# Twenty of the low-part subtractions of a decoder trunk's weights issued on GpSimd instead of VectorE

## The chip, the cores and the metric

The kernel runs on one core of one Trainium2 chip. The metric is the device time of one execution in microseconds (us); the time of a kernel is the median of its runs. One execution is also recorded by the hardware profiler, and the profile's spans, groups and waits come from that one.

Five queues work side by side: TensorE (PE, with its weight loads as PEld), VectorE (DVE), ScalarE (ACT), GpSimd (POOL) and SyncE (SP), which here only issues transfers. Each queue runs its instructions strictly in its own order; semaphores order them between queues.

## What is computed

The input is a residual stream of 512 tokens by 1024 channels. Layer 0 mixes by causal average pooling, layer 1 by stick-breaking attention with 16 heads of 64 channels; each layer adds a squared-ReLU MLP (1024 to 4096 to 1024), with an RMS norm before and after each part. The part that the change touches is layer 1's attention:

```python
h = rms_norm(x, mix_pre_g[layer])
q = jnp.matmul(h, w_q[j])                        # 1024 x 1024
kv = jnp.matmul(rms_norm(x, kv_norm_g), w_kv)    # k and v, 1024 x 1024 each
a[t, s] = sigmoid(z) * prod_{s<j<t} (1 - sigmoid(z_tj))   # z = q k^T / 8, strictly causal
m = jnp.matmul(o, w_o[j])                        # o = a v, 1024 x 1024
```

All data are float32.

## The kernel before, in words

**Split products.** TensorE's operands are held as two parts of a narrower float format (fp32r): `hi` is the value rounded by ScalarE's cast, and `lo` is the value minus `hi`. A product is three matmuls: hi x hi, hi x lo and lo x hi (`mm3`, lines 208 to 211, and `up_block`, lines 530 to 536). So every weight tile has to be split before TensorE can use it.

**How a weight comes in.** `weight` (lines 106 to 121) makes one tile of 128 x 1024. It takes one of two `raw` buffers, has SyncE issue the load (512 KB, L108), for the q, k and v weights has GpSimd multiply the tile in place by a norm gain in two halves of 128 x 512 (L130), has ScalarE cast `hi` (L118), and has an engine subtract `lo = raw - hi` (L120). That engine is VectorE, unless the weight's key is in the set `ON_POOL` (L43, looked up in `make`, L154), in which case it is GpSimd. In the kernel before, the set holds four of the first MLP's up weights: 0, 1, 2 and 4. The `raw` buffer is free for the load after next only when its `lo` has been made. The parts `h` and `l` lie in four buffers each (L150).

**What orders the work.** Weights are queued in the order in which they will be used (`want`, lines 171 to 184), and `fill` (lines 157 to 162) makes the next one at set places of the program if fewer than four are waiting. In attention, `weight` queues its cast behind ScalarE's latest instruction of the main work and its `lo` behind VectorE's latest (`later`, lines 110 to 120): `issue_after(ins)` places behind `ins` those instructions of the block that run on the engine of `ins`. A planner (`schedule_with_timeline_sim`, L887) then fixes the order of each queue when the kernel is compiled, from durations that it assumes; nothing is reordered at run time.

**The attention stage.** Its program order is written out by hand in `ATT_ORDER` (lines 49 to 53). Eight pairs of heads pass through it, overlapped: P projects keys and queries of a pair (two `up_block`s of 24 matmuls, then `kl` and `q` low parts on VectorE, L694 and L703); S multiplies queries by keys, has ScalarE make two sigmoids `u` and `w` (L746, L750), VectorE scan `u` into `e` (L752, 128 x 1280) and multiply `w` by `e` (L756); T has TensorE transpose `w` (L770) and splits the result into `ah` and `al` (L188, L189); A multiplies by the values (L780) and sums into `o` (L786, L787), which is split as `ohl`. V makes values (L209 to L211 with `xnh`, then L654, L655) and O multiplies finished pairs by the o weights (L209 to L211 with `ohl`). The order of the weights in attention is: v0, k0, q0, k1, q1, v1, k2, q2, k3, q3, o0, o1, k4, q4, v2, k5, q5, k6, q6, v3, k7, q7, o2 to o7; each v is two tiles.

The scan reads two SBUF tensors, and so do `w x e`, the `ohl` split and `lo = raw - hi`; the other VectorE operations of the stage read one operand from PSUM.

Of the kernel before, what the change touches and what calls it, by code (L numbers as in the profile page):

```python
# [25 lines left out]
PAIRS = HEADS // 2  # L26
# [14 lines left out]


ON_POOL = {("up", 0, j) for j in (0, 1, 2, 4)}  # L43

# [15 lines left out]
def trunk(ctx, tc, x, consts, gcol, grow, pw, wup, wdn, wq, wk, wv, wo, out):  # L62
# [43 lines left out]
    def weight(src, tiles, scaled=None, on=nc.vector):  # L106
        raw = wts.tile([P, D], F32, tag="raw", bufs=2, name=name("raw"))
        nc.sync.dma_start(raw, src)  # L108

        def later(engine):  # L110
            return tc.issue_after(behind[engine].ins) if engine in behind else nullcontext()

        if scaled is not None:
            with later("pool"):
                scaled(raw)
        hi, lo = tiles
        with later("act"):
            nc.scalar.copy(hi, raw)  # L118
        with later("dve"):
            on.tensor_tensor(out=lo, in0=raw, in1=hi.bitcast(F32), op=ALU.subtract)  # L120
        return hi, lo
# [19 lines left out]
    def place(k):  # L141

        if k[0] == "dn":
            return [dn_pool[0].tile([P, D], F32R, tag="w", bufs=8, name=name(x)) for x in "hl"]
        if k == ("o", 6):
            both = att_pool[0].tile([P, 2, D], F32R, tag="v", bufs=2, name=name("w"))
            return [both[:, 0], both[:, 1]]
        if k == ("o", 7):
            return [att_pool[0].tile([P, NSEG], F32R, tag="w", bufs=2, name=name(x))[:, :D] for x in "hl"]
        return [wts.tile([P, D], F32R, tag=f"w{x}", bufs=4, name=name(x)) for x in "hl"]  # L150

    def make():
        k, src, scaled = queue.pop(0)
        on = nc.gpsimd if k in ON_POOL else nc.vector  # L154
        made[k] = weight(src, place(k), scaled, on)
# [735 lines left out]
```

## Time and profile before

| | us |
|---|---|
| median of three runs | 994.51 (992.58 to 997.41) |
| the profiled execution, its own time | 996.64 |
| its span, first to last instruction | 994.8 |
| TensorE busy in the span | 954.4 |
| VectorE busy | 780.6 |
| ScalarE busy | 557.0 |
| GpSimd busy | 252.2 |

The profiled execution took 996.64 us, of which 994.8 us lie between its first and its last instruction. Busy time is the time in which an engine had an instruction under way. A row of the timeline gives start and duration in us, the engine, the line of the kernel, the operation, output and inputs with their shapes, and in brackets how long the engine sat idle before it and what ended that. A row of a group gives the count, the busy time in all and the mean of one in ns. `in_wk`, `in_wq`, `in_wv` and `in_wo` are the weights in memory; `l` and `h` are the parts of a weight; `ps` is any PSUM tile.

### The profile page before, as it was taken

Reading aid. Unit: us, or ns where it says so; the run is one execution under the profiler, and the core shown is the slowest. Engines: PE = TensorE matmul, PEld = TensorE weight load, DVE = VectorE, ACT = ScalarE, POOL = GpSimd, SP = SyncE. Lnnn points to the kernel's source line nnn. Section 1 sums busy time; section 2 is a strip of 40 time slices with the busy share of each in tenths; the row PEclk is TensorE's granted clock in tenths of the full one; section 3 lists DMA queues with packets and bytes.
Section 4 is the critical chain, followed back from the end, with each engine's and each line's share of the span. In section 5 each row is a group of like instructions: output and inputs, shape, how many; then the busy total and the mean of one; then the engine's idle time right before and its main releaser. Section 6 shows DMA issues by size and latency. Waiting matters only on the chain.

```text
span 994.8 us, 12988 instructions
## 1 busy us (share of the span) xinstructions
PE 954.4 (96%) x4823; PEld 810.8 (82%) x4823; DVE 780.6 (78%) x1067; ACT 557.0 (56%) x1005; POOL 252.2 (25%) x238
## 2 busy tenths in 40 slices
PE   7898999999999999999999999989999999999997
PEld 5896888888888888888788988788888888888886
DVE  5987788878877747488688889989778878888636
ACT  5656546456455446566667576658556455464532
POOL 1642202112021147241252300436212021121103
PEclk8998999999999999999999999999999999999999
DMA  7254323323232230112222221144323233231202
GB/s 267 85 162 135 106 86 107 109 103 106 85 111 81 85 127 22 62 45 64 64 73 69 64 72 65 65 148 149 110 102 111 84 125 105 85 127 64 64 22 85
DMA packets 26991, 94.50 MB, mean 95 GB/s; under 512 B 3120, under 2 KB 3504, under 8 KB 26928
## 3 DMA queue, kind: packets, MB, share of 16 engines
q1 hardware_dynamic: 26928, 93.68, 28.2%
q8 instruction: 38, 0.62, 0.2%
q14 instruction: 25, 0.20, 0.1%
HBM read 91.57 MB, written 2.10 MB: 94 GB/s over the span
## 4 chain that ended last, share of the span: by engine, by line
PE 76%; DVE 8%; ACT 4%; POOL 3%; issue 2%; DMA 1%; POOLq 0%; DVEq 0%; ACTq 0%
PE ps L456 26%; PE ps L535 13%; PE ps L536 13%; PE ps L534 13%; PE ps L209 3%; PE ps L210 2%; PE ps L211 2%; DVE e L752 2%; PE ps L780 1%; DVE l L120 1%; PE ps L770 1%; POOL y L234 1%; DMA xn<-in_wdn 1%; ACT h L118 1%; DVE x L240 1%
## 5 line engine op out<-in xcount | busy, mean ns | idle before, releaser
L535 PE MATMUL ps<-xnl,h 128*128 128x512 f32 (+1 forms) x712 | 262.0, 369 | 4.1 <-DVE xnl L189 4.1
L536 PE MATMUL ps<-xnh,l 128*128 128x512 f32 (+1 forms) x712 | 262.1, 369 | 0.5 <-DVE l L120 0.5
L534 PE MATMUL ps<-xnh,h 128*128 128x512 f32 (+1 forms) x712 | 261.0, 369 | 0.0
L120 DVE TENSOR_TENSOR l<-raw,h 128x1024 fp32r<-128x1024 f32 x101 | 128.8, 1276 | 48.5 <-ACT h L118 48.3
L456 PE MATMUL ps<-w,s 128*128 128x512 f32 x672 | 163.4, 394 | 2.1 <-ACT s L188 1.5
L535 PEld LDWEIGHTS ps<-xnl,h 128*128 128x128 f32 x712 | 134.8, 189 | 26.1 <-DVE xnl L189 4.3
L536 PEld LDWEIGHTS ps<-xnh,l 128*128 128x128 f32 x712 | 134.8, 189 | 22.8 <-DVE l L120 0.7
L456 PEld LDWEIGHTS ps<-w,s 128*128 128x128 f32 x672 | 127.2, 190 | 31.1 <-ACT s L188 2.7
L534 PEld LDWEIGHTS ps<-xnh,h 128*128 128x128 f32 x712 | 134.2, 190 | 21.9
L473 DVE TENSOR_TENSOR y<-ps,y 128x512 f32<-128x512 f32 x180 | 120.1, 688 | 40.5 <-PE ps L456 39.3
L118 ACT CAST h<-raw 128x1024 fp32r<-128x1024 f32 x105 | 110.4, 1053 | 63.9 <-PE ps L535 32.4
L456 PE MATMUL ps<-w,r 128*128 128x512 f32 x504 | 124.3, 390 | 2.4 <-DVE r L189 2.4
L188 ACT CAST w<-t 128x512 fp32r<-128x512 f32 x112 | 69.2, 622 | 80.8 <-PE ps L456 61.0
L456 PEld LDWEIGHTS ps<-w,r 128*128 128x128 f32 x504 | 94.7, 188 | 22.4 <-DVE r L189 2.8
L404 POOL TENSOR_TENSOR s<-r,r 128x256 f32<-128x256 f32 x28 | 28.2, 1008 | 323.9 <-ACT r L490 323.9
L130 POOL TENSOR_TENSOR raw<-raw,gc 128x512 f32<-128x512 f32 x48 | 69.9, 1477 | 145.7 <-DMA raw<-in_wv 68.9
L188 ACT CAST w<-xn 128x512 fp32r<-128x512 f32 x56 | 34.9, 624 | 90.1 <-PE ps L456 80.0
L189 DVE TENSOR_TENSOR w<-t,w 128x512 fp32r<-128x512 f32 x112 | 76.5, 705 | 0.7 <-ACT w L188 0.7
L188 ACT CAST s<-s 128x512 fp32r<-128x512 f32 x56 | 34.6, 620 | 45.6 <-POOL s L405 37.6
L189 DVE TENSOR_TENSOR s<-s,s 128x512 fp32r<-128x512 f32 x56 | 42.5, 763 | 22.0 <-ACT s L188 17.5
L189 DVE TENSOR_TENSOR r<-r,r 128x512 fp32r<-128x512 f32 (+1 forms) x60 | 47.2, 789 | 11.7 <-ACT r L188 11.6
L752 DVE TENSOR_TENSOR_SCAN e<-u,begin 128x1280 f32<-128x1280 f32 x16 | 47.5, 2968 | 8.7 <-ACT u L746 8.5
(138 smaller groups left out, 1577.9 us busy)
## 6 DMA issues: line engine op xcount, KB each, us to landing
raw<-in_wup SPq DMA_DIRECT2D x64, 512.0 KB, 3.5
xn<-in_wdn SPq DMA_DIRECT2D x42, 512.0 KB, 3.6
spare<-in_wdn SPq DMA_DIRECT2D x14, 512.0 KB, 4.1
raw<-in_wdn SPq DMA_DIRECT2D x8, 512.0 KB, 3.5
raw<-in_wv SPq DMA_DIRECT2D x8, 512.0 KB, 3.4
raw<-in_wk SPq DMA_DIRECT2D x8, 512.0 KB, 3.5
raw<-in_wq SPq DMA_DIRECT2D x8, 512.0 KB, 3.5
raw<-in_wo SPq DMA_DIRECT2D x8, 512.0 KB, 3.5
```

Of the source, the lines that this page charges most:

```text
L118: nc.scalar.copy(hi, raw)
L120: on.tensor_tensor(out=lo, in0=raw, in1=hi.bitcast(F32), op=ALU.subtract)
L130: nc.gpsimd.tensor_tensor(out=v[:, h], in0=v[:, h], in1=g[:, h].broadcast_to((P, n // 2, D // n)), op=ALU.mult)
L188: latest["act"] = nc.scalar.copy(hi, src)
L189: latest["dve"] = nc.vector.tensor_tensor(out=lo, in0=src, in1=hi.bitcast(F32), op=ALU.subtract)
L209: nc.tensor.matmul(dst, ah, bh, start=start, stop=False)
L456: nc.tensor.matmul(bank, r[:, a], w_[:, NS[b]], start=start and q == 0 and k == 0, stop=q == 1 and k == 2, skip_group_check=True,)
L473: nc.vector.tensor_tensor(out=part, in0=bank, in1=part, op=ALU.add)
L534: nc.tensor.matmul(pu[:, cols], wh[:, k, :], xnh[:, k, cols], start=k == 0, stop=False)
L535: nc.tensor.matmul(pu[:, cols], wh[:, k, :], xnl[:, k, cols], start=False, stop=False)
L536: nc.tensor.matmul(pu[:, cols], wl[:, k, :], xnh[:, k, cols], start=False, stop=k == KC - 1)
L752: nc.vector.tensor_tensor_scan(out=e[:, ::-1], data0=u[:, 1:][:, ::-1], data1=begin[:, ::-1], initial=0.0, op0=ALU.mult, op1=ALU.max,)
```

## The change

One line adds twenty keys to the set: the k and q weights 1 to 7 (fourteen tiles) and the o weights 0 to 5 (six tiles). The `lo` of each is then issued on GpSimd's queue, in which the gain multiplications also stand, and no longer on VectorE's. Keys k0, q0, o6, o7, all v weights and the MLP weights are left as they are. Since the block around the subtraction names VectorE's latest instruction, it places nothing in front of a subtraction that runs on GpSimd.

```diff
@@ -41,6 +41,8 @@
 
 
 ON_POOL = {("up", 0, j) for j in (0, 1, 2, 4)}
+
+ON_POOL |= {(x, i) for x in "kq" for i in range(1, PAIRS)} | {("o", i) for i in range(6)}
```

## The prediction

> **What bounds the kernel now.** I read the shares of the engines first, then the attention stage as one stretch of the table by stage (its columns after the length: PE, PEld, DVE, ACT and POOL busy, each with its count, then clock and DMA), since the twenty weights are split between 409 and 614 us, and then TensorE's waits in that stretch (total, times, longest).
>
> ```profile
> PE 954.4 (96%) x4823; PEld 810.8 (82%) x4823; DVE 780.6 (78%) x1067; ACT 557.0 (56%) x1005; POOL 252.2 (25%) x238
> ```
> ```profile
> 405.00:632.00 227.00, 217.77 (x1251) 190.28 (x1249) 186.94 (x192) 145.39 (x288) 55.69 (x37) 0.99 0.21 69
> ```
> ```profile
> PE ps L209 <- DVE kl L694: 1.9, 2, 1.4
> PE ps L780 <- ACT ah L188: 1.7, 1, 1.7
> PE ps L780 <- DVE al L189: 1.6, 2, 0.9
> PE ps L738 <- DVE q L703: 1.0, 1, 1.0
> ```
>
> TensorE bounds the kernel: 96% of the span, and 217.8 of the stage's 227.0 us. So 9.2 us can be won there at most, however much VectorE is relieved. The longest waits end with VectorE, but not with a weight's subtraction: with main work that stands in the same queue. VectorE is busy for 186.9 us of the stage and GpSimd for 55.7 us, so there is room on GpSimd; the question is what of VectorE's relief reaches TensorE's gaps.
>
> **What is removed and added.** First the subtraction on either engine (min, median and max in ns):
>
> ```profile
> L120 DVE TENSOR_TENSOR l<-raw,h x101: 1193/1225/2304, 16.1 to 952.4; 128x1024 fp32r<-128x1024 f32 x101
> ```
> ```profile
> L120 POOL TENSOR_TENSOR l<-raw,h x4: 2366/2466/2807, 25.2 to 65.3; 128x1024 fp32r<-128x1024 f32 x4
> ```
>
> VectorE loses 20 x 1.225 = 24.5 us. GpSimd gets 20 x 2.466 = 49.3 us and stands at 55.7 + 49.3 = 105 us of 227. Neither sum is TensorE's.
>
> **The two engines stop each other**, and this decides how much of the 24.5 us VectorE keeps:
>
> ```profile
> 647.43 2.30 DVE L120 TENSOR_TENSOR l<-raw,h 128x1024 fp32r<-128x1024 f32 x1
> ```
> ```profile
> 646.93 1.72 POOL L249 TENSOR_TENSOR y<-x,spare 128x512 f32<-128x512 f32 x1 [0.87 <-DVE x L240]
> ```
>
> GpSimd's operation ran to 646.93 + 1.72 = 648.65. VectorE's subtraction, recorded from 647.43, ended at 649.73: 1.08 us after GpSimd let go, nearly the whole of its own 1.2. It had stood still until then. The Trainium skill states this as a rule (SBUF — State Buffer, section "SBUF: two separate sides"): a GpSimd operation and a VectorE operation with two SBUF inputs share one port pair, held for a whole instruction, and the loser fully blocks. The trace agrees in these two rows.
>
> What this costs VectorE in the stage today is the mean above the median (means of the stage first, then medians):
>
> ```profile
> L752 DVE TENSOR_TENSOR_SCAN e<-u,begin 128x1280 f32<-128x1280 f32 x16 | 47.5, 2968 | 8.7 <-ACT u L746 8.5
> L120 DVE TENSOR_TENSOR l<-raw,h 128x1024 fp32r<-128x1024 f32 x29 | 37.9, 1310 | 9.2 <-ACT h L118 9.1
> L756 DVE TENSOR_TENSOR w<-w,e 128x1280 f32<-128x1280 f32 x16 | 26.1, 1633 | 0.8
> ```
> ```profile
> L752 DVE TENSOR_TENSOR_SCAN e<-u,begin x16: 2807/2825/3486, 421.2 to 605.7; 128x1280 f32<-128x1280 f32 x16
> ```
> ```profile
> L756 DVE TENSOR_TENSOR w<-w,e x16: 1472/1490/2081, 424.7 to 609.0; 128x1280 f32<-128x1280 f32 x16
> ```
> ```profile
> L130 POOL TENSOR_TENSOR raw<-raw,gc x36: 1035/1042/3553, 414.3 to 567.7; 128x512 f32<-128x512 f32 x36
> ```
>
> Scans 16 x 0.143 = 2.3 us, products 16 x 0.143 = 2.3, subtractions 29 x 0.085 = 2.5: 7.1 us for 36 x 1.042 = 37.5 us of gain multiplications, 0.19 us for each us of GpSimd. For 49.3 us more that is 9.4 us. A wait for the rest of one operation also grows with its length, 2.466 against 1.042, so at most 9.4 x 2.37 = 22 us. VectorE keeps between 24.5 - 22 = 2 and 24.5 - 9.4 = 15 us.
>
> **Where it meets TensorE's gaps.** `lo` can start on GpSimd where ScalarE has ended `hi`:
>
> ```profile
> L118 ACT CAST h<-raw x29: 1042/1051/1216, 408.2 to 626.6; 128x1024 fp32r<-128x1024 f32 x29
> ```
>
> Of the twenty that are moved I found most to end where VectorE works on PSUM, which a subtraction on GpSimd doesn't disturb; there 1.2 us leave a queue that TensorE doesn't wait for, worth 0. Five places have a gap of TensorE or a scan beside them.
>
> *First, 518 to 525 us* (k5 and q5): the largest gaps, as pieces of the chain of waits and then on TensorE.
>
> ```profile
> 519.09 1.23 DVE l L120
> ...
> 521.67 1.05 ACT h L118
> 522.75 1.23 DVE l L120
> ```
> ```profile
> 523.65 0.49 PE L780 MATMUL ps<-ah,v 128*128 128x512 f32 x1 [1.67 <-ACT ah L188]
> 525.08 0.50 PE L780 MATMUL ps<-al,v 128*128 128x512 f32 x1 [0.94 <-DVE al L189]
> ```
>
> Both 1.23 us leave this chain, 2.5 at most, and no scan runs here. Late next is ScalarE, whose `ah` casts stand behind its cast of q5's `hi`: only the first subtraction moves that. TensorE gets 0.7 to 2.5 us; I take 1.3, one subtraction and a little.
>
> *Second, 413 to 418 us* (q1).
>
> ```profile
> 414.44 1.95 DVE l L120
> 416.42 0.70 DVE q L703
> 417.17 0.58 issue
> 417.75 1.05 ACT h L118
> ```
> ```profile
> 414.27 3.02 POOL L130 TENSOR_TENSOR raw<-raw,gc 128x512 f32<-128x512 f32 x2 [16.76 <-DMA raw<-in_wv]
> ```
>
> L703 stands behind the subtraction, and the wait of 1.0 us on L703 above is this one; it can go. But GpSimd's gain multiplication of the next weight began at 414.27, just when q1's `lo` would take GpSimd. If `lo` is first, the next `hi` (the cast at 417.75) is up to 2.47 - 1.23 = 1.2 us late, and ScalarE's sigmoids and the scans behind it. Between 1.0 won and 1.2 lost I take 0.
>
> *Third, 447 to 454 us* (q2): the one place where TensorE waits for the `lo` of a weight that is moved at more than 0.2 us.
>
> ```profile
> 446.59 1.22 ACT L118 CAST h<-raw 128x1024 fp32r<-128x1024 f32 x1
> ```
> ```profile
> 448.94 3.32 DVE L752 TENSOR_TENSOR_SCAN e<-u,begin 128x1280 f32<-128x1280 f32 x1
> 452.19 1.19 DVE L120 TENSOR_TENSOR l<-raw,h 128x1024 fp32r<-128x1024 f32 x1
> ```
> ```profile
> 453.44 0.50 PE L536 MATMUL ps<-xnh,l 128*128 128x512 f32 x1 [0.51 <-DVE l L120]
> ```
>
> `hi` is there at 447.8. If GpSimd has its turn before the scan, `lo` is early and 0.5 us goes; if the scan is first, `lo` runs from 452.3 to 454.7 instead of to 453.4, and 1.3 us is lost. I take the middle, 0.4 lost.
>
> *Fourth, 476 to 487 us* (o0, o1).
>
> ```profile
> 476.21 1.05 ACT L118 CAST h<-raw 128x1024 fp32r<-128x1024 f32 x1
> ```
> ```profile
> 478.42 0.67 DVE L189 TENSOR_TENSOR ohl<-o,ohl 128x512 fp32r<-128x512 f32 x1
> 479.00 1.49 DVE L756 TENSOR_TENSOR w<-w,e 128x1280 f32<-128x1280 f32 x1
> ```
> ```profile
> 485.68 0.50 PE L210 MATMUL ps<-l,ohl 128*128 128x512 f32 x1 [0.21 <-DVE l L120]
> ```
>
> o0's `hi` ends at 477.3, inside a scan; GpSimd's turn comes when that ends, at 478.4, and pushes the product back by 2.47 us, while 1.22 us leave the queue behind it. TensorE takes o1's `lo` at once, so its 2.47 instead of 1.22 us adds up to 1.2. At worst 1.4 us is lost; at best the 1.2 us that leave VectorE are won, less a later o1, 0.7. I take 0.6 lost, as both longer durations stand in its way.
>
> *Fifth, 605 to 611 us* (o4).
>
> ```profile
> 605.90 1.05 ACT L118 CAST h<-raw 128x1024 fp32r<-128x1024 f32 x1 [3.19 <-PE ps L211]
> ```
> ```profile
> 605.70 2.82 DVE L752 TENSOR_TENSOR_SCAN e<-u,begin 128x1280 f32<-128x1280 f32 x1
> ```
> ```profile
> 610.55 0.66 PE L770 MATMUL ps<-ident,w 128*128 128x128 f32 x4 [0.17 <-DVE w L756]
> ```
>
> `hi` ends at 607.0, again inside a scan that runs to 608.5. GpSimd then has 608.5 to 611.0, so the product behind it ends 1.49 us later, at 612.4, and TensorE, which was served at 610.55, waits 1.9 us more; the subtractions of o4 and o5, which no longer stand behind the product, give back 1.2 to 2.4. Between 1.2 won and 0.6 lost I take 0.3 lost.
>
> **Transfers.** A `raw` buffer is freed by `lo` (SyncE's own waits):
>
> ```profile
> SPq L108 <- DVE l L120: 195.1, 27, 19.6
> ```
>
> All loads of the stage hang on L120. Where `lo` starts right behind `hi`, the load after next goes out 1.2 us later; where VectorE's queue held it (q2: 4.4 us from `hi` to `lo`), earlier. The cover is the four weights made ahead, so I cost it at 0; without cover it is 1.2 us a weight. The gain multiplications now share their queue with a `lo` in front; beyond the second place I cost that at 0 too, as GpSimd is free for 122 of 227 us.
>
> **Sum:** -1.3 + 0 + 0.4 + 0.6 + 0.3 = 0.0 us, with ends at -(2.5 + 1.0 + 0.5 + 0.7 + 1.2) = -5.9 and -0.7 + 1.2 + 1.3 + 1.4 + 0.6 = +3.8. The profiled execution stays at its 996.6, which is 2.1 us above the median; against the median of 994.5 the ends are 988.6 and 998.3. I put the time at 995.0, half a us up, because GpSimd's queue stands in front of ScalarE's casts in more places than these.
>
> **Rivals.** *Slower: GpSimd's turn comes inside the scans.* The mechanism is the standstill above, which the skill's rule of the whole instruction makes general. Scan, product, scan and product of a pair of heads offer a turn at each boundary; a `lo` that takes one costs the chain 2.47 us where 1.23 leave it, so 1.24 each and 2.5 a pair with both weights. It decides where the second product ends less than 2.5 us ahead of TensorE's transposes. With three pairs like the one at 610 us, and the bad end of the third place: 3 x 2.5 + 1.3 = 8.8 us, 1003.3. For it: scans already reach 3486 and multiplications 3553 ns. Against: TensorE waits for a product 0.2 us in the whole stage, so most pairs have a lead.
>
> *Faster: the subtractions were the last straw for VectorE.* All good ends, 5.9 us: 988.6; all gaps closed, 9.2 us: 985.3. For it: most of the long waits end with VectorE. Against: ScalarE or a scan is late next in four of the five places.
>
> *The planner orders the queues anew*, as an instruction has changed its engine. No row has a price for that. It widens both rivals: at best to the closed gaps, -9.2 us, at worst I take the 9.4 us that VectorE's new waits may reach by their average price, plus the 2 us by which single runs lie off the median, +11.
>
> The skill also advises against the change as such (GPSIMD Engine Reference, section "Engine selection": elementwise work with two inputs belongs on VectorE, GpSimd taking about twice as long). The rows agree on the factor, 2466 against 1225 ns; by the advice alone the sum would be a loss, by busy time GpSimd stays far from a bound.
>
> **Chances.** Within 0.5% of 994.5, about what a measurement of this kernel can tell from no change (989.5 to 999.5): 0.40, the forecast. Slower: 0.38, at 1003.3. Faster: 0.22, at 988.6. The range for 8 in 10 runs from 986.5, a little above all gaps closed, to 1006, 994.5 + 11.
>
> **What would show it.** Right: L120 on VectorE falls from 101 to 81 and on GpSimd rises from 4 to 24, with a mean above 2.5 us; scans and products have larger means than 2968 and 1633; the gaps at k5 and q5 shrink by about 1 us, those beside o0 and o4 grow. Wrong: TensorE's idle time in the stage is under 5 us (the faster rival), or over 14 us with waits that end in L756 or L770 (the slower one); if they end in `h`, `l` or a sigmoid, GpSimd's queue has become what the weights wait for.

## The result, and the profile after

The changed kernel takes 998.46 us (median of 12 runs, 996.60 to 1003.85) against 994.36 us for the kernel before (12 runs, 991.80 to 998.28). The ratio is 1.0044, with a 95% interval of 1.0025 to 1.0063: slower by 4.1 us. That lies inside the range of the prediction and just inside its band of 0.5% around no change, but twelve runs of each do tell it from no change. Timed again later, the same kernel stood at 1.0057 [1.0041, 1.0073]. The profiled execution took 998.91 us, 2.3 us more than that of before.

The shares of the engines on the page of the changed kernel, then the attention stage as one stretch of the table by stage (PE, PEld, DVE, ACT and POOL busy, each with its count, then clock and DMA):

```profile
PE 952.8 (96%) x4823; PEld 810.2 (81%) x4823; DVE 761.7 (76%) x1047; ACT 556.5 (56%) x1005; POOL 305.2 (31%) x258
```
```profile
405.00:632.00 227.00, 213.21 (x1216) 186.35 (x1215) 165.81 (x169) 144.31 (x286) 105.94 (x57) 0.98 0.21 68
```

VectorE was relieved of 186.94 - 165.81 = 21.1 us in the stage, and GpSimd stands at 105.9 us, as worked out. But TensorE did less in the same 227 us: its idle time rose from 9.2 to 227 - 213.21 = 13.8 us. The length of the stage is taken from here on from the matmul that ends TensorE's wait for the norm (`xnh`, at 397.82 us, before at 399.39) to the one that ends its wait for the next norm (`xnl`): it is 255.9 us, before 252.7.

TensorE's waits in the stage show where (total, times, longest, in us). Lines of the changed kernel are two higher than before: L122 is the subtraction, L772 and L782 the matmuls that were L770 and L780.

```profile
PE ps L538 <- POOL l L122: 3.6, 1, 3.6
PE ps L211 <- DVE kl L696: 3.5, 3, 1.2
PE ps L772 <- DVE w L758: 1.6, 2, 1.3
PE ps L212 <- POOL l L122: 1.4, 1, 1.4
PE ps L772 <- DVE q L705: 1.1, 1, 1.1
PE ps L536 <- ACT w L752: 1.0, 1, 1.0
```

Two of these are new in kind: TensorE waits for a low part that GpSimd makes, for 3.6 and 1.4 us. The first alone is larger than any wait in the stage before. The chain of waits around it (start, length, what), in the changed kernel:

```profile
439.45 3.46 DMA raw<-in_wk
...
444.56 3.55 POOL raw L132
448.12 3.57 POOL l L122
451.69 0.04 issue
451.73 0.80 PE ps L538
452.53 0.43 PE ps L536
...
454.66 0.32 PE ps L538
454.98 0.23 PE ps L536
```

The wait is for q2's low part (L122). That subtraction stood behind a gain multiplication (L132) of the *next* weight, k3, in GpSimd's queue. Both were stretched: the second half of the multiplication took 3.55 us, where the median of before was 1.042, and the subtraction 3.57 instead of 2.47. VectorE's scan and product ran beside them. The kernel before had k3's multiplication stretched as well, where no subtraction stood behind it on GpSimd:

```profile
444.24 5.34 POOL L130 TENSOR_TENSOR raw<-raw,gc 128x512 f32<-128x512 f32 x2 [1.87 <-DMA raw<-in_wk]
```

Behind the gap TensorE's matmuls take 0.43 us a piece until 454.98, and then 0.23: the granted clock fell to half.

Where TensorE stands in the stage is seen from the first matmul of each S step, in us after the matmul at which the stage's length begins (from the timelines of one execution each):

| pair | 0 | 1 | 2 | 3 | 4 | 5 | 6 | 7 |
|---|---|---|---|---|---|---|---|---|
| before | 17.8 | 41.2 | 68.1 | 99.7 | 126.4 | 151.1 | 175.2 | 196.7 |
| after | 15.1 | 38.0 | 69.4 | 102.2 | 130.6 | 156.3 | 180.3 | 201.4 |
| lo_first | 15.1 | 38.1 | 64.2 | 98.6 | 125.5 | 149.6 | 173.5 | 195.6 |
| lo_first_half | 16.6 | 39.6 | 65.7 | 97.7 | 125.0 | 149.2 | 173.2 | 195.5 |
| no_lo | 15.1 | 38.2 | 64.4 | 94.1 | 119.9 | 144.5 | 168.6 | 189.9 |

The changed kernel is 3.2 us *ahead* at pair 1, and 1.3 us late at pair 2: 4.5 us are lost at one weight. A further 3.9 us go by pair 5, and little from there. (Of the 3.2 us ahead, some 1.7 us are a stretch at half clock that the recorded execution of before had at 400 us and this one had not, 14 us at a mean clock of 0.88. So part of the 4.5 us may belong to the two executions and not to the change.)

### The profile page after: what moved, and what is told of

It reads as the page before. It is cut to its first block, busy times and chain, and to the rows that moved or that the text cites. A ratio compares the mean times of both kernels' runs of the same rounds, so it can differ in the third digit from the quotient of the medians.

```text
span 997.1 us, 12991 instructions
## 1 busy us (share of the span) xinstructions
PE 952.8 (96%) x4823; PEld 810.2 (81%) x4823; DVE 761.7 (76%) x1047; ACT 556.5 (56%) x1005; POOL 305.2 (31%) x258
## 4 chain that ended last, share of the span: by engine, by line
PE 68%; DVE 9%; POOL 6%; issue 5%; ACT 4%; DMA 3%; POOLq 0%; DVEq 0%; ACTq 0%
PE ps L458 26%; PE ps L537 12%; PE ps L538 12%; PE ps L536 12%; POOL raw L132 2%; POOL l L122 2%; PE ps L211 1%; PE ps L212 1%; PE ps L213 1%; DVE w L758 1%; DVE l L122 1%; PE ps L782 1%; ACT h L120 1%; POOL y L236 1%; ACT xn L194 1%
## 5 line engine op out<-in xcount | busy, mean ns | idle before, releaser
L458 PEld LDWEIGHTS ps<-w,s 128*128 128x128 f32 x672 | 126.4, 189 | 30.0 <-ACT s L190 2.7
L122 DVE TENSOR_TENSOR l<-raw,h 128x1024 fp32r<-128x1024 f32 x81 | 104.0, 1285 | 46.2 <-ACT h L120 46.2
L132 POOL TENSOR_TENSOR raw<-raw,gc 128x512 f32<-128x512 f32 x48 | 68.2, 1442 | 80.3 <-DVE l L122 23.9
L122 POOL TENSOR_TENSOR l<-raw,h 128x1024 fp32r<-128x1024 f32 x24 | 64.6, 2693 | 76.2 <-ACT h L120 76.2
L405 POOL TENSOR_TENSOR s<-r 128x256 f32<-128x256 f32 x28 | 32.3, 1152 | 86.3 <-ACT r L492 73.0
```

What stands on the lines that cost most here:

```text
L132: nc.gpsimd.tensor_tensor(out=v[:, h], in0=v[:, h], in1=g[:, h].broadcast_to((P, n // 2, D // n)), op=ALU.mult)
L405: nc.gpsimd.tensor_tensor(out=s3, in0=r1[:, lo], in1=r1[:, hi], op=ALU.subtract)
L458: nc.tensor.matmul(bank, r[:, a], w_[:, NS[b]], start=start and q == 0 and k == 0, stop=q == 1 and k == 2, skip_group_check=True,)
```

## The experiments

All kernels were timed in five rounds beside the kernel before on the same chip; ratios are to that kernel. The kernels of one group ran on one chip.

The theory (A in the expectations): what is lost is lost where TensorE waits for a low part that GpSimd makes late, above all q2's, and the order of GpSimd's queue makes it late. The rival (B): the loss is spread, as GpSimd's subtractions stop VectorE by their presence, whoever waits for their results.

**Is it q2, and what makes q2 late?** The first puts q2's subtraction back on VectorE, the second moves q2's alone, the third keeps the change and orders GpSimd's queue, the fourth leaves the twenty subtractions out.

q2_back, on the changed kernel:

```diff
+ON_POOL -= {("q", 2)}
```

> The changed kernel with one of its twenty subtractions, that of q2, put back on VectorE; GpSimd's queue is otherwise in the same order. Theory A (one place): of the 4.1 us that the change cost, the 3.6 us in which TensorE waited for q2's low part, with the clock's dip behind it, are nearly all; so 3 to 5 us come back, to 0.995 to 0.997 of the changed kernel (994 to 995.5 us), and the wait on that line is 0.5 us as before. Theory B (many small standstills between GpSimd and VectorE, the slower rival): one of twenty gives back 0.2 us, and the waits move to the next places; 997.5 to 998.5 us.

Measured: 995.97 against 996.15 us, ratio 1.0000 [0.9987, 1.0014]: as A expects against the kernel before. The queues of TensorE and ScalarE hold the same order as in the changed kernel and VectorE's has one subtraction more, so nothing but this weight differs. Nineteen weights on GpSimd cost nothing and win nothing; the twentieth brings the loss. In the recorded execution, which took 999.83 us and has a stretch at half clock at 400 us as before's has, the wait at q2 fell to 1.14 us, not to the 0.5 that A expected:

```profile
PE ps L539 <- DVE l L123: 1.1, 1, 1.1
```

q2_only, on the kernel before:

```diff
+ON_POOL |= {("q", 2)}
```

> The kernel before with only the subtraction of q2 put on GpSimd. Theory A: this one alone costs most of it, 2.5 to 4 us (997 to 998.5 us), with TensorE waiting for the low part of q2 for 3 us or more. Theory B: 1.24 us at most, hidden or not: 994.4 to 995.6 us.

Measured: 997.08 us, ratio 1.0009 [0.9994, 1.0025]. Alone, q2 costs about 1 us, less than A expected and, with an interval that holds 1, not told from nothing, although here too its subtraction stands behind k3's gain multiplication (GpSimd's timeline: start, duration, what):

```profile
441.53 5.42 POOL L132 TENSOR_TENSOR raw<-raw,gc 128x512 f32<-128x512 f32 x2 [1.79 <-DMA raw<-in_wk]
446.92 4.86 POOL L122 TENSOR_TENSOR l<-raw,h 128x1024 fp32r<-128x1024 f32 x1
```

TensorE waited 1.54 us for it, since it came to q2 at 52.1 us of the stage and not at 50.4 as in the changed kernel. The other nineteen had brought TensorE forward, and q2's late part took that away and more.

lo_first, on the changed kernel: a subtraction on GpSimd becomes the instruction behind which later gain multiplications are queued.

```diff
-            on.tensor_tensor(out=lo, in0=raw, in1=hi.bitcast(F32), op=ALU.subtract)
+            made_lo = on.tensor_tensor(out=lo, in0=raw, in1=hi.bitcast(F32), op=ALU.subtract)
+        if on is nc.gpsimd and gate[0]:
+            behind["pool"] = latest["pool"] = made_lo
```

> The changed kernel, with each gain multiplication in attention placed behind the subtraction before it in GpSimd's queue (three pairs change places, q2's and k3's among them). If the order of GpSimd's queue is what makes q2 late (A), q2's subtraction starts right at the end of its cast or of the scan then running, some 3 us earlier than now; the wait of 3.6 us shrinks to under 1.5 us, and 2 to 4 us come back (994.5 to 996.5 us), unless the multiplications that are now later hold up ScalarE's casts (then 997 to 999 us, with waits of ScalarE on raw). Theory B: the standstills are as many as before, 997.5 to 999 us.

Measured: 994.70 us, ratio 0.9986 [0.9970, 1.0002], all twenty weights still on GpSimd. The same place in GpSimd's timeline:

```profile
444.27 2.46 POOL L122 TENSOR_TENSOR l<-raw,h 128x1024 fp32r<-128x1024 f32 x1 [4.83 <-ACT h L120]
446.70 5.80 POOL L134 TENSOR_TENSOR raw<-raw,gc 128x512 f32<-128x512 f32 x2
```

q2's low part is ready at 446.7, k3's multiplication, stretched to 5.80 us, comes behind it, and TensorE no longer waits there. The edit binds every gain multiplication in the stage, and the planner moved some rows of the other queues with it, so its gain isn't that of q2 alone; q2_back, which touches nothing else, gives back nearly as much.

no_lo, on the kernel before: the low parts of the twenty weights are zeros, made once, and `raw` is freed by the cast.

```diff
+        if on is None:
+            return hi, zero
...
-        on = nc.gpsimd if k in ON_POOL else nc.vector
+        on = None if k in ZERO_LO else nc.gpsimd if k in ON_POOL else nc.vector
```

> The kernel before without the twenty subtractions: TensorE takes a tile of zeros in place of these low parts, so part of each product is left out, and raw is free as soon as the cast is done. GpSimd gets nothing new. This prices VectorE's relief of 24.5 us by itself. If VectorE's queue held TensorE up (the faster rival), 4 to 8 us go, 986.5 to 990.5 us. If scans and ScalarE are late next, as my sum had it, 2 to 4 us go, 990.5 to 992.5 us. If the relief is worth nothing, 993.5 to 995.5 us.

Measured: 986.56 us, ratio 0.9909 [0.9891, 0.9926]. This prices the relief, with the earlier release of `raw` in it, at 9 us, where the prediction's good ends made 5.9. The stage of the changed kernel and this one differ in TensorE's idle time by 10 us:

```profile
405.00:632.00 227.00, 223.07 (x1269) 194.61 (x1268) 170.18 (x186) 150.71 (x303) 61.05 (x43) 0.99 0.23 70
```

**Is the lost relief GpSimd's work or the lateness of its results?** In the next group TensorE reads zeros in place of the twenty low parts, while the subtractions still run, on VectorE or on GpSimd, and free `raw` as before. So no one waits for the low parts. The changed kernel itself ran beside them.

after_again, the changed kernel without an edit:

> The changed kernel itself, once more, beside the other three, since the kernel before came out at 994.4 us on one chip and at 996.2 us on another and the differences here are under 1%. Both theories: 1.0025 to 1.0063 of the kernel before. If it comes out under 1.002, nothing may be read into q2_back at 1.000.

Measured: 1000.31 against 994.52 us, ratio 1.0057 [1.0041, 1.0073]. The loss repeats, and so does the wait for q2 (3.58 us).

lo_unread, on the kernel before, and pool_unread, on the changed kernel (only the set differs):

```diff
+        if k in UNREAD:
+            made[k] = made[k][0], zero
```

> The kernel before, with its subtractions on VectorE, but TensorE takes a tile of zeros in place of the twenty low parts, so part of each product is left out and nobody waits for these subtractions but the raw buffers. It tells what in no_lo's 0.991 came from zeros and from not waiting for the low parts, and what from the relief of VectorE's queue. If the relief is it, this stays at 0.998 to 1.000. If the zeros (cooler matmuls, a higher clock) or the low parts' lateness are it, 0.991 to 0.995.

> The changed kernel, with the twenty subtractions on GpSimd, but TensorE takes a tile of zeros in place of these low parts (part of each product is left out). What remains of the change is GpSimd's work, its queue in front of the casts and its standstills with VectorE; what is gone is TensorE's wait for low parts. Theory A (late low parts, of q2 and o1): 0.991 to 0.995, most of VectorE's relief comes through. Theory B (standstills and GpSimd's queue eat the relief): 0.997 to 1.001, as VectorE's scans and ScalarE's casts are late all the same.

Measured: lo_unread 995.71 us, ratio 1.0011 [0.9999, 1.0023]; pool_unread 993.79 us, ratio 0.9983 [0.9971, 0.9995]. The first says that zeros on TensorE are worth nothing, so no_lo's 1% is relief. The second lies in the range of B. Then the account by ratios is: relief, from 1.0011 to 0.9909, is worth 1.0%. GpSimd's subtractions by their presence take back 0.74% (0.9909 to 0.9983): standstills of VectorE, casts that wait behind GpSimd's queue and later loads together, which no run parts. TensorE's waits for late low parts take back another 0.6 to 0.7% (0.9983 to 1.0044 or 1.0057; the queues of pool_unread hold nearly the order of the changed kernel). no_lo ran on another chip than the others, so its two shares are rough. The stage by itself says the same: in one execution each it took 251.2 us in lo_unread, 244.8 in no_lo, 249.9 in pool_unread and 255.9 in the changed kernel, which makes 6.4 us of relief, 5.1 of presence and 6.0 of lateness. Neither theory holds alone; each half takes back more than half of the gain, so the two together turn it into a loss.

lo_first_o, which is lo_first with three of the o weights back on VectorE:

```diff
+ON_POOL -= {("o", 0), ("o", 1), ("o", 4)}
```

> lo_first, and the subtractions of o0, o1 and o4 put back on VectorE: seventeen stay on GpSimd. In lo_first TensorE still waited 1.41 us for o1's low part, 1.25 us beside o0 and 1.26 us beside o4. Theory A (places decide): these shrink to what they were in the kernel before (0.2, 0.5 and 0.2 us), 2 to 3 us below lo_first, 0.994 to 0.997 of the kernel before. Theory B (VectorE's relief and its standstills in sum decide): three fewer standstills and three subtractions more on VectorE, about nothing, 0.997 to 1.000.

Measured: 996.59 us, ratio 1.0028 [1.0012, 1.0044]. The waits at o0 and o1 fell as A said (1.25 to 0.52 and 1.41 to 0.21 us), but A failed as a total. A new wait of 2.89 us came at 608.63, behind this stretch of VectorE's timeline:

```profile
603.46 1.48 DVE L761 TENSOR_TENSOR w<-w,e 128x1280 f32<-128x1280 f32 x1
604.86 3.38 DVE L123 TENSOR_TENSOR l<-raw,h 128x1024 fp32r<-128x1024 f32 x1
608.16 0.41 DVE L660 TENSOR_TENSOR v<-ps,v 128x256 fp32r<-128x256 f32 x1
```
```profile
603.99 3.17 POOL L123 TENSOR_TENSOR l<-raw,h 128x1024 fp32r<-128x1024 f32 x1 [14.35 <-ACT h L121]
```

Two subtractions of neighbouring weights, one on each engine, are ready together. GpSimd's runs to 607.16; VectorE's, 1.2 us long by itself, ends 1.1 us after that. The split between engines sets them against each other. The planner also ordered TensorE's and VectorE's queues anew, and the second MLP took 345.3 us in place of 343.4, so this run says nothing of the o weights alone.

**What would a smaller obstacle give?** The last group.

short_lo, which is lo_unread with VectorE's twenty subtractions cut to 64 of their 1024 columns:

```diff
-            on.tensor_tensor(out=lo, in0=raw, in1=hi.bitcast(F32), op=ALU.subtract)
+            on.tensor_tensor(out=lo[:, :n], in0=raw[:, :n], in1=hi[:, :n].bitcast(F32), op=ALU.subtract)
```

> lo_unread, with the twenty subtractions on VectorE cut from 1024 columns to 64: the instruction, its place in the queue and the release of raw stay, only some 1.1 us of VectorE's time each, 22 us in all, go (TensorE takes zeros for these low parts, so part of each product is left out). lo_unread came out at 1.0011 and no_lo at 0.9909; the 1% between them is either VectorE's time or the raw buffers and casts that are no longer tied to VectorE's queue. Theory R (VectorE's time): 0.990 to 0.993. Theory S (raw freed by the cast, so earlier loads): 0.997 to 1.001.

Measured: 989.72 against 993.58 us, ratio 0.9960 [0.9945, 0.9974]. The stage is as short as no_lo's (244.4 and 244.8 us), though `raw` is still freed only when VectorE's queue comes to it: the worth of the relief lies in VectorE's time, mostly not in earlier loads. As a total it misses: from lo_unread's 1.0011 it wins 0.5%, half of what no_lo won. The second MLP, which took 344.8 us in place of 342.7, makes up 0.2% of the difference; where the rest lies is open, as the three kernels ran on three chips.

raw3, the kernel before with three `raw` buffers, and lo_first_raw3, lo_first with three:

```diff
-        raw = wts.tile([P, D], F32, tag="raw", bufs=2, name=name("raw"))
+        raw = wts.tile([P, D], F32, tag="raw", bufs=3, name=name("raw"))
```

> The kernel before with three raw buffers in place of two, all subtractions on VectorE. Loads go out one weight earlier and hang less on the subtraction. Theory S: 0.992 to 0.997. Theory R: 0.998 to 1.002, as VectorE's work is the same.

> lo_first with three raw buffers. In lo_first each gain multiplication waits for the subtraction before it, and the load for a third buffer no longer does. If GpSimd's queue in front of ScalarE's casts still costs something by late loads, 0.994 to 0.997 of the kernel before; if it is GpSimd's own time and the standstills, 0.998 to 1.000, as lo_first.

Measured: 1002.09 us, ratio 1.0085 [1.0069, 1.0101], and 1004.11 us, ratio 1.0102 [1.0086, 1.0118]. Both tests are spoiled: of raw3's loss 5.6 us lie behind the stage, in the second MLP (348.3 against 342.7 us), whose weights use the same buffers. Whether the hold of `raw` matters inside the stage stays open; the stage grew from 252.7 to 254.2 us, and from lo_first's 250.1 to 254.7, with the loads ordered anew.

lo_first_half, which is lo_first with the subtractions on GpSimd from k2 on (18 of the 20) cut in two halves of 512 columns:

```diff
+            for n in NS if on is nc.gpsimd and gate[0] else [slice(0, D)]:
+                made_lo = on.tensor_tensor(out=lo[:, n], in0=raw[:, n], in1=hi[:, n].bitcast(F32), op=ALU.subtract)
```

> lo_first with each of the subtractions on GpSimd from k2 on cut into two of 512 columns. A VectorE operation with two SBUF operands then waits for at most 1.25 us of subtraction, not 2.47. If the length of GpSimd's operation is what the standstills cost, as my range for VectorE's kept time supposed, the means of scans and products fall and the time to 0.994 to 0.997; against that stands a second start for each (0.1 us) and that two halves can be parted by a scan, so that the low part is ready later: then 0.998 to 1.002.

Measured: 989.90 us, ratio 0.9965 [0.9951, 0.9979]: 0.35% or 3.5 us faster than the kernel before, with all twenty weights on GpSimd. The stage takes 249.9 us, and TensorE's idle time in it is 8.0 us. Its wait for o1's low part, first in lo_first and then here (TensorE's timeline, the wait in brackets):

```profile
483.48 0.50 PE L214 MATMUL ps<-l,ohl 128*128 128x512 f32 x1 [1.41 <-POOL l L122]
```
```profile
482.73 0.50 PE L215 MATMUL ps<-l,ohl 128*128 128x512 f32 x1 [0.32 <-POOL l L123]
```

It fell from 1.41 to 0.32 us, and the wait for a product at 610 us from 1.26 to 0.17. The scans' mean fell only from 3060 to 3018 ns, the products' from 1842 to 1789 and that of the `ohl` split from 1346 to 1112, some 3.4 us of VectorE in all. But other waits of TensorE grew, and as a whole the stage is hardly shorter than lo_first's 250.1 us, with 8.3 us of idle time. lo_first ran on another chip, and the intervals of the two overlap: that the halves add to what the order gave is not shown.

## Why the prediction was right and wrong

**The time and the sign of the forecast.** "No change" came out at +0.44%, in the forecast's case and at its upper edge. The sum of 0.0 us is in truth about +4.6 us of TensorE's idle time in the stage (13.8 less 9.2 us). So the forecast held by the width of its band, and not because its sum was right; that is luck. Place by place, by TensorE's gaps in the two timelines:

**First place (k5, q5), -1.3 forecast: right in size.** The gaps there fell from 3.26 to 2.10 us. But late next is VectorE's own main work, not ScalarE's `ah`:

```profile
524.96 0.41 PE L772 MATMUL ps<-ident,w 128*128 128x128 f32 x2 [1.10 <-DVE q L705]
526.37 0.80 PE L782 MATMUL ps<-ah,v 128*128 128x512 f32 x1 [1.00 <-DVE v L657]
```

**Second place (q1), 0 forecast: better.** The wait of 0.99 us went and nothing took its place; the next one, for `kl`, fell from 1.43 to 1.05 us. GpSimd's subtraction ran 411.36 to 413.76, with the gain multiplication behind it, and no sigmoid was late.

**Third place (q2), 0.4 lost forecast, 1.3 at worst: this is the step that failed.** It lost 3.05 us of waiting (0.51 to 3.56) and then a stretch at half clock. The prediction asked only whether the subtraction would have its turn before or after the scan. It did not ask what stands in front of it in GpSimd's queue, and under "Transfers" it costed that queue at 0, "as GpSimd is free for 122 of 227 us". Free time on average does not help an instruction that is queued behind one which takes 5.07 us beside the scan. `hi` was ready at 443.04, the moment at which k3's multiplication began:

```profile
443.04 5.07 POOL L132 TENSOR_TENSOR raw<-raw,gc 128x512 f32<-128x512 f32 x2 [3.62 <-DMA raw<-in_wk]
448.08 3.60 POOL L122 TENSOR_TENSOR l<-raw,h 128x1024 fp32r<-128x1024 f32 x1
```

q2_back and lo_first show this cause from both sides: take this subtraction off GpSimd's queue or put it in front, and the loss is gone. The program's block that gives a subtraction its place works on VectorE's queue; no statement kept k3's multiplication behind q2's subtraction on GpSimd's.

A second thing is easily overlooked. Counted from the stage's beginning, q2's low part was ready at 53.9 us, and before at 54.0: it came no later than VectorE had made it. TensorE came to it at 50.3 us, and before at 53.5. The wait grew because TensorE's work ran ahead and the low part did not: some 1.4 us of the lead were won at q1 and `kl`, and some 1.7 us are the stretch at half clock that only the recorded execution of before had. So this place handed back what the second had won. The sum adds the places as if each stood alone; a gain at one brings the need for the next weight forward. In lo_first the low part was ready at 47.8 us.

**Fourth place (o0, o1), 0.6 lost forecast, 1.4 at worst: in its bounds.** The gaps rose from 1.44 to 2.65 us, 1.2 lost. GpSimd's turn did come at the end of the scan, but what it pushed back was first the `ohl` split, which took 2.82 us instead of 0.67; these are VectorE's, GpSimd's and TensorE's rows:

```profile
478.11 2.82 DVE L191 TENSOR_TENSOR ohl<-o,ohl 128x512 fp32r<-128x512 f32 x1
```
```profile
477.02 3.37 POOL L122 TENSOR_TENSOR l<-raw,h 128x1024 fp32r<-128x1024 f32 x1 [12.84 <-ACT h L120]
```
```profile
485.01 0.47 PE L211 MATMUL ps<-h,ohl 128*128 128x512 f32 x1 [1.25 <-DVE kl L696]
...
487.59 0.50 PE L212 MATMUL ps<-l,ohl 128*128 128x512 f32 x1 [1.40 <-POOL l L122]
```

**Fifth place (o4), 0.3 lost forecast: mechanism right, balance a little better.** The product stood still as described, 3.04 us instead of 1.49, and the wait behind it grew from 0.17 to 1.26 us; the two gaps behind it, 0.81 us for `v` and 0.63 for `al`, are gone, so that the place won 0.35 us.

```profile
611.61 3.04 DVE L758 TENSOR_TENSOR w<-w,e 128x1280 f32<-128x1280 f32 x1
```
```profile
610.09 6.80 POOL L122 TENSOR_TENSOR l<-raw,h 128x1024 fp32r<-128x1024 f32 x2 [12.30 <-ACT h L120]
```

**The other fifteen places, 0 forecast: 3.1 us lost.** New gaps stand at 504, 517, 546 and 548 us (1.04, 0.43, 0.34 and 1.25 us). The first is the chain of which the prediction said that it put half a us on for it, GpSimd's queue in front of ScalarE's casts; in ScalarE's and TensorE's rows:

```profile
501.44 1.05 ACT L120 CAST h<-raw 128x1024 fp32r<-128x1024 f32 x1 [1.48 <-POOL raw L132]
```
```profile
504.27 0.50 PE L536 MATMUL ps<-xnh,h 128*128 128x512 f32 x1 [1.04 <-ACT w L752]
```

A cast that waits for a multiplication holds the sigmoids behind it. For the other three no run undoes a single cause.

**Standstills of VectorE, 9.4 to 22 us forecast: mis-sized.** The means of the stage after the change:

```profile
L754 DVE TENSOR_TENSOR_SCAN e<-u,begin 128x1280 f32<-128x1280 f32 x16 | 47.6, 2978 | 10.0 <-ACT u L748 9.8
L758 DVE TENSOR_TENSOR w<-w,e 128x1280 f32<-128x1280 f32 x16 | 27.3, 1704 | 0.7
...
L122 DVE TENSOR_TENSOR l<-raw,h 128x1024 fp32r<-128x1024 f32 x9 | 13.0, 1456 | 5.8 <-ACT h L120 5.8
...
L191 DVE TENSOR_TENSOR ohl<-o,ohl 128x512 fp32r<-128x512 f32 x8 | 9.9, 1239 | 1.5 <-ACT ohl L190 1.5
```

The last of them before:

```profile
L189 DVE TENSOR_TENSOR ohl<-o,ohl 128x512 fp32r<-128x512 f32 x8 | 6.3, 786 | 0.7 <-ACT ohl L188 0.7
```

Against before the scans cost 0.1 us more and the products 1.2; the nine subtractions left stand 2.1 us above their median, where the 29 stood 2.5 above; and the `ohl` split, which the prediction left out, costs 9.9 - 6.3 = 3.6 us more. That is about 0.1 + 1.2 - 0.4 + 3.6 = 4.5 us for 49 us more of GpSimd. In the prediction VectorE was to keep 2 to 15 of its 24.5 us; it kept some 20 (21.1 by the table by stage, whose cut is fixed in time). The average price of the gain multiplications does not carry over: those start when a load lands, at any time, whereas a subtraction starts when ScalarE's cast ends, which for most weights is while VectorE reads PSUM. That last is argued from the places that I found, not shown by a run.

**The bound of 9.2 us: not passed.** By its ratio no_lo won 0.91%, some 9.0 us. In its profile 5.3 us of the idle time went (9.2 to 3.9), and the stage was 7.9 us shorter. It also lacks the stretch at half clock that the recorded execution of before had at 400 us, some 1.7 us which the table counts as busy; the changed kernel's execution lacks it too, so this is no mark of the relief. Where the rest of the 9 us lies is not shown.

**The rivals.** The slower rival named standstills in the scans, 1.24 us each. It had the sign and not the place: the scans' mean moved from 2968 to 2978 ns, while the `ohl` split and the products stood still. The faster rival, that the subtractions were the last straw for VectorE, is true of the cause and false of the result: relief was worth some 9 us in no_lo, but not by this way of giving it. The planner did order the queues anew, a few rows of TensorE's and more of ScalarE's and VectorE's; q2_back has the same new order at no loss, so that order by itself is not what costs. Of the signs of being right, the counts and means came true (L122 stands 81 times on VectorE and 24 times on GpSimd), the scans' by 10 ns only, and so did the gaps at k5 and q5, at o0, and before o4's product. Of the signs of being wrong the last came true as well: waits that end in `l`, at 13.8 us of idle time, just under the 14 that were named.

## What to carry to other kernels

Before an operation is moved to an engine with room, write down that engine's queue around each place: what stands directly in front, what that waits for, and whether it is stretched there by what runs beside it. A share of busy time does not answer this. If a low part is needed soon, let it go ahead of the preparation of the next weight, as lo_first does. Cutting it in pieces shortened single waits in lo_first_half, but not the stage. And do not add up gains place by place as if they were independent: an engine that gains time reaches the next result earlier, and that result has to come earlier too.

Value the relief and the move apart: a kernel without the operation shows what relief is worth (here 6.4 us of the stage, and 1.0% of the time), one with it on the new engine but its result unread shows what its presence costs (5.1 us, 0.74%), and the difference to the real one is lateness (6.0 us, 0.6 to 0.7%). Such shares are rougher than their digits: short_lo puts the relief at 6.8 us of the stage, but at 0.5% of the time.

## What the runs showed of the hardware

**Short gaps can be followed by half clock.** Behind the 3.56 us gap, matmuls of 512 columns started 0.43 us apart instead of 0.23 for about 3.3 us. In the windows of 10 us the granted clock from 450 to 460 is 0.83 (mean clock, then DMA), before it was 1.00; 0.17 of 10 us is a further 1.7 us that TensorE loses, by estimate:

```profile
450.00:460.00 10.00, 8.27 (x38) 6.98 (x39) 4.65 (x9) 4.54 (x8) 6.05 (x4) 0.83 0.17 54
```
```profile
450.00:460.00 10.00, 9.49 (x56) 8.03 (x55) 9.87 (x10) 6.77 (x13) 2.04 (x2) 1.00 0.17 52
```

The Trainium skill (TensorE: Matmul & The Clock Gate, section "HAM oscillation — how this bites in real kernels") asks for no idle gaps above about 3.4 us. The gap at q2 agrees. But in before a gap of 1.83 us that ended at 399.4 and gaps of 1.67 and 0.94 us by 525, and in the changed kernel gaps of 1.10 and 1.00 us by 526, were followed by such a stretch as well (mean clocks of 0.88 from 396 to 410 and of 0.83 from 520 to 530), while a gap of 1.80 us at 398 in the changed kernel was not. By the rows here, gaps of half that length can do it and need not. The same page of the Trainium skill (section "What's actually happening") describes the window of the clock gate as one that runs free of the kernel, so that the moment of a change depends on where in it the matmuls fall. That could explain the difference; no run here tests it. The runs of one kernel spread with the clock: the changed kernel's ran from 996.60 us at a mean clock of 0.991 to 1003.85 at 0.978.

**The standstill falls on either engine.** GpSimd's two gain multiplications took 5.07 us beside a scan and 2.04 elsewhere in the same execution; VectorE's `ohl` split took 2.82 instead of 0.67 beside a subtraction on GpSimd. The prediction had priced it on VectorE alone, and the dearest case was on GpSimd, which here was the engine that TensorE waited for.
